# Where the mixers' PSUM banks lie, and how their first normed tiles are placed

## The chip, the cores and the metric

The kernel runs on one core of one Trainium2 chip. The metric is the device time of one execution in microseconds (us), here the median of three runs. Engines are named as in the profile: PE (TensorE matmuls, PEld their weight loads), DVE (VectorE), ACT (ScalarE), POOL (GpSimd), SP (SyncE, which here issues almost all DMAs).

## The reference

One decoder block over 1040 tokens (16 meta tokens and 1024 of the input) of width 1024: a half-step SwiGLU feed-forward, a mixer stage, a second half-step SwiGLU, a final norm.

```python
h = h + 0.5 * _swiglu(_rmsnorm(h, ffn1_norm[l]), ffn1_w_gu[l], ffn1_w_down[l])
u = _rmsnorm(h, mix_norm[l])
aq, ak, av, az, abeta, aalpha, bcols, ga, gb = jnp.split(u @ w_in[l], _offsets(IN_SIZES), axis=-1)
o_a = _deltanet_branch(...)
o_b = _rwkv7_branch(...)
merged = jax.nn.sigmoid(ga) * o_a + jax.nn.sigmoid(gb) * o_b
h = h + merged @ w_out[l]
h = h + 0.5 * _swiglu(_rmsnorm(h, ffn2_norm[l]), ffn2_w_gu[l], ffn2_w_down[l])
return _rmsnorm(h, final_norm)[:, N_META:]
```

The two branches are a gated DeltaNet in chunks and an RWKV-7 time mixing, with 8 and 16 heads.

## The kernel before

Activations lie transposed: 8 tiles h0 to h7 of 128 features by 1040 tokens. Every matrix product is made of three fp32r products: each operand is split into a high part (ACT copies it, line 163) and a low part (a subtraction, line 164, on DVE unless another engine is named), and high x high, high x low and low x high are summed in PSUM. The order of instructions on each engine is fixed at compile time by a list scheduler with its own timing model; an engine then executes its queue strictly in order, waiting on semaphores.

**First feed-forward, ffn1.** The down products go through 7 rounds r of Strassen-like forms. A round has 11 forms (a `form` tile: 128 x 520, high and low part), loaded from the DRAM buffer frm, and 4 products m (pd, line 707), each added to h by DVE (line 714). `Hidden` keeps a list `slots` of the places in which the 77 forms lie in turn. `even` and `odd` are places in the buffers of the gate-up stage (11, 21, t2 and t3, 22, t4, t1: four each). The last round (r = 6) is made in two passes, first 264 columns of all four m, then 256. `before_last`, called after round 5, loads that round's last forms into the freed weight-sum buffer wsum, loads the constants ck, and opens on the right side of SBUF the pools `up` (the mixers' inputs uk) and `un` (norm temporaries). `after` runs behind each product of the last round: squares and their sums for the mixers' norm, of segment 0 (528 tokens: nsq summed on DVE) and segment 1 (512 tokens: nsq summed on POOL). After the first pass the segment-0 sum is reduced by a matmul with ones (nps, line 338) and becomes the scale nrs (lines 340 and 341, ACT). Behind each product of the second pass, two tiles nt = h * gain * nrs (line 871, DVE) are made and split into uk (lines 163 and 164): the low part on POOL for odd k, on DVE for even k.

**Mixers, middle.** PSUM has 8 banks. ffn1 has `mm` with 3 pairs of banks (0 to 5) for products and `mx` with banks 6 and 7. `middle` closes these, opens `ch` with two banks (for the chains of a head pair, and for the head pair's final norms: cs, lines 1213 to 1234), and then `main_banks` opens `mm` and `mx` in what is left: 2 pairs and 2 banks, later, from the seventh head pair on, 3 single banks and 3. Memory is allocated from the lowest address unless a pool says `side="right"`; with `reuse_waits="tile"` a new tile waits for the users of whatever lay in its place. The first projections (pp, line 307) take the eight uk in order, for 272 columns and then 256. POOL clears the mixers' buffers (line 1006 on), behind its ffn1 work.

**Between the mixers and the second feed-forward, ffn2.** `fill` makes the output product (pwo, line 307; ho, line 1101) of the first half while the last head pair is still in its chains, and splits seven of the second half's eight inputs (uk from mr). The eighth comes from `finish` of the last head pair: cs of oa and yb, ro and rg (ACT), yb, uk. Then `ffn2` opens `mm` with 6 banks and `mx` with 2 and makes the second half's pwo, each weight tile of which lies in one of two buffers (tag "w"), in the course of its own first norm (nsq, lines 320 and 327).

Of the kernel before, what the change touches and what calls it, by code (L numbers as in the profile page):

```python
# [8 lines left out]
F32 = mybir.dt.float32  # L9
F32R = mybir.dt.float32r  # L10
# [3 lines left out]
P = 128  # L14
D = 1024
KD = D // P
# [8 lines left out]
ROW = lambda n: -(-n // 64) * 64  # L25
# [16 lines left out]
HK = KD // 2  # L42
HF = NF // 2
# [4 lines left out]
LAST = len(FORMS) - 1  # L48
# [62 lines left out]
def build(tc, nc, a):  # L111

    ctx = ExitStack()
    with ctx:
# [39 lines left out]
        ffn1(g)  # L154
        middle(g)
        ffn2(g)


# [216 lines left out]
def first_half(g, hs, gname, n, b, on_pe):  # L375

    src = lambda k: hs[k][:, :n]
    rs = rstd(g, src, n, on_pe)
    yield
    for k in range(KD):  # L380
        g.nc.vector.scalar_tensor_tensor(src(k), src(k), g.V(gname, k), rs, op0=ALU.mult, op1=ALU.mult)
        bk = b["21" if k >= HK else "11"][:, k % HK]
        split(g, src(k), bk[:, 0, :], bk[:, 1, :])
    yield
# [89 lines left out]
def weight_tiles(g):  # L474

    new = lambda pool, name, k: pool.tile([P, 2, k, P], F32R, name=name, tag=name)
    g.wq = [g.wp.tile([P, 2, KD, P], F32R, name="w", tag="w", bufs=WB) for _ in range(2)]
    g.wq += [new(g.wx, "w22", HK), new(g.wx, "w22b", HK), new(g.wx, "w24", KD)]
# [143 lines left out]
class Hidden:  # L622
# [46 lines left out]

    def arrange(self, spare, last):  # L670
        e, o = self.even, self.odd
        self.slots = e[:HF] + (o[:HF] + e[:HF]) * 2 + o[:HF] + o[HF:] + [spare] + last

    def load(self, upto, done):
        while len(self.loads) < min(upto, len(self.slots)):
# [93 lines left out]
def ffn1(g):  # L769
    tc, nc = g.tc, g.nc  # L770
    n = T // 2
    with ExitStack() as ctx:
        right = ExitStack()
        early = ExitStack()
        pools = {}
        for names, pool in ((("11", "21", "t2"), early.enter_context(
                tc.tile_pool(name="f1a", bufs=1, side="right", reuse_waits="tile"))),
                (("t3", "22", "t4", "t1"), ctx.enter_context(tc.tile_pool(name="f1b", bufs=1, reuse_waits="tile")))):
            pools.update({x: pool for x in names})
        b = {x: p.tile([P, HK, 2, ROW(n)], F32R, name=f"b{x}", tag=f"b{x}", bufs=1)[:, :, :, :n]  # L780
             for x, p in pools.items()}
        b["12"] = b["t4"]
        g.wx = right.enter_context(tc.tile_pool(name="wx", bufs=1, side="right", reuse_waits="tile"))
        g.ga = right.enter_context(tc.tile_pool(name="ga", bufs=1, side="right", reuse_waits="tile"))
        with tc.tile_pool(name="f1n", bufs=1, reuse_waits="tile") as sp:
            hs = [sp.tile([P, T], F32, name=f"h{k}") for k in range(KD)]
            for s in range(2):
                for k in range(KD):
                    sl = slice(s * n, (s + 1) * n)
                    (nc.sync if s or k % 2 else nc.scalar).dma_start(hs[k][:, sl], g.a["hT"][k][:, sl])  # L790
                if not s:
                    weight_tiles(g)
                    q0 = whole(g, 1, 0, 0, g.wq[0], g.wq[1])
                    w0 = next(q0)
            q1 = whole(g, 1, 0, 1, g.wq[4], g.wq[2], g.wq[3])
            w1 = next(q1)
            first = first_half(g, hs, "g1", n, b, True)
            next(first)
            next(q0)
            next(first)  # L800
            next(q0)
            start(g, 1, hs, "g1", n, b, (w0, w1), q1)
            gu = g.gate_up
        hidden = Hidden(g, n, pools, 1)
        wp = ctx.enter_context(tc.tile_pool(name="ws", bufs=1, reuse_waits="tile"))
        g.wsum = wp.tile([P, HK, HF, P], F32, name="wsum", tag="wsum", bufs=1)
        with tc.tile_pool(name="gs", bufs=1, reuse_waits="tile") as sp:
            gu.send((hidden.ahead(), sp))
        right.close()
        xctx = ExitStack()  # L810
        sp = ctx.enter_context(tc.tile_pool(name="f1", bufs=1, reuse_waits="tile"))
        hs = {k: sp.tile([P, T], F32, name=f"h{k}") for k in (3, 7, 2, 6, 5, 1, 0, 4)}
        spare = sp.tile([P, 2, ROW(n)], F32R, name="form")[:, :, :n]
        hidden.odd = hidden.places("t3", "22", "t4", "t1")
        hidden.arrange(spare, [])
        g.wthird = ctx.enter_context(tc.tile_pool(name="wd", bufs=1, reuse_waits="tile"))
        hooks = K()

        def residual(k, half):
            sl = slice(half * n, half * n + n)  # L820
            in_turn(g, hs[k][:, sl], g.a["hT"][k][:, sl])

        hooks.before = lambda r, m: residuals(r, m, residual)

        def before_last():
            early.close()
            t = wp.tile([P, 5, 2, ROW(n)], F32R, name="form", tag="wsum", bufs=1)
            hidden.slots += [t[:, i, :, :n] for i in range(5)]
            hidden.load(len(hidden.slots), LAST)
            for x in ("t3", "22"):  # L830
                t = pools[x].tile([P, 3, 2, CHUNKS[0][1], P], F32R, name="w", tag=f"b{x}", bufs=1)
                g.held += [t[:, i] for i in range(3)]
            g.upctx = ExitStack()
            cp = g.upctx.enter_context(tc.tile_pool(name="ckp", bufs=1, side="right", reuse_waits="tile"))
            g.ck = cp.tile([P, NSB - P + 32], F32, name="ck")[:, : NSB - P]
            in_turn(g, g.ck, g.a["ck"][:, P:NSB])
            g.up = g.upctx.enter_context(tc.tile_pool(name="up", bufs=1, side="right", reuse_waits="tile"))
            g.un = xctx.enter_context(tc.tile_pool(name="un", bufs=1, side="right", reuse_waits="tile"))
            with ExitStack() as after:
                for x in g.silus:  # L840
                    after.enter_context(tc.issue_after(x.ins))
                nc.scalar.preload_act_table_set("natural_log_exp_and_others")
            hooks.rms = [Rms(g, lambda: g.un.tile([P, 528], F32, name="nsq", tag="nsq", bufs=4), n,
                             add_on=nc.gpsimd if s else None) for s, (_, n, _) in enumerate(SEGS)]
            hooks.todo = []
            for s in range(2):
                for k in range(HK, KD):
                    squares(s, k)

        def squares(s, k):  # L850
            t0, sn, _ = SEGS[s]
            hooks.rms[s].add(hs[k][:, t0 : t0 + sn])
            nc.sync.dma_start(g.hdr[s][k], hs[k][:, t0 : t0 + sn])

        def after(r, m, s):
            if r < LAST:
                if r == LAST - 1 and m == HK - 1:
                    before_last()
                return
            squares(s, m)  # L860
            if m == HK - 1:
                rs = g.un.tile([P, 528], F32, name="nrs", tag="nrs", bufs=2)
                hooks.rms[s].finish(rs)
                if s == 0:
                    g.u = []
                    hooks.todo = [(k, rs) for k in range(KD)]
                else:
                    nc.sync.dma_start(g.rdr, rs[:, :FULL])
            for k, rs in hooks.todo[: 2 * s]:
                t = g.un.tile([P, 528], F32, name="nt", tag="nt", bufs=2)  # L870
                nc.vector.scalar_tensor_tensor(t, hs[k][:, SEGS[0][0] :], g.V("gm", k), rs, op0=ALU.mult, op1=ALU.mult)
                g.u.append(u_tile(g, t, nc.gpsimd if k % 2 else None))
            del hooks.todo[: 2 * s]

        hooks.after = after
        down(g, hs, 1, n, hidden, hooks)
        xctx.close()


def ffn2(g):  # L880
    tc, nc = g.tc, g.nc
    n = FULL
    main_banks(g, 1, 6, 8)
    with ExitStack() as ctx:
        right = ExitStack()
        bp = ctx.enter_context(tc.tile_pool(name="f2b", bufs=1, reuse_waits="tile"))
        pools = {x: bp for x in ("11", "21")}
# [25 lines left out]
        hidden = Hidden(g, n, pools, 2)  # L913
# [7 lines left out]
        g.wthird = ctx.enter_context(tc.tile_pool(name="wd", bufs=1, reuse_waits="tile"))  # L921
        hidden.odd = hidden.places("t3", "22", "t4", "t1")
        e = hidden.even
        hidden.arrange(e[HF], e[4:9])
        hooks = K()
        hooks.rows = {}

# [55 lines left out]
def middle(g):  # L983
    tc, nc = g.tc, g.nc
    g.mmctx.close()
    with ExitStack() as ctx:
        g.ch = ctx.enter_context(tc.tile_pool(name="ch", bufs=2, space=bass.MemoryType.PSUM, reuse_waits="tile"))
        ctx.callback(g.mmctx.close)
        ep = lambda name, bufs=1: ctx.enter_context(tc.tile_pool(name=name, bufs=bufs, reuse_waits="tile"))
        g.ms = ep("ms")  # L990
# [86 lines left out]
def u_tile(g, src, eng=None):  # L1077

    n = src.shape[-1]
    uk = g.up.tile([P, 2, ROW(528)], F32R, name="uk", tag="uk", bufs=8)[:, :, 528 - n : 528]  # L1080
    split(g, src, uk[:, 0, :], uk[:, 1, :], eng)
    return uk
# [836 lines left out]
```

## Time and profile before

| | us |
|---|---|
| median of three runs | 3006.02 (3003.01 to 3011.42) |
| profiled execution | 3009.62 |
| its span on the core | 3007.6 |
| ffn1 | 0 to about 708 |
| mixers | about 714 to 2290 |
| ffn2 | about 2290 to 3008 |

The view of stretches (busy time of each engine, then the mean granted clock of PE, the share of the DMA engines and GB/s) puts the passages beside the long stages:

```profile
690.00:735.00 45.00, 38.28 (x283) 36.44 (x282) 28.45 (x33) 22.36 (x35) 20.58 (x29) 0.89 0.31 98
...
870.00:1485.00 615.00, 589.54 (x7374) 508.03 (x7373) 472.59 (x1193) 353.01 (x738) 31.60 (x136) 0.99 0.30 77
...
2220.00:2350.00 130.00, 122.25 (x872) 95.20 (x871) 73.86 (x124) 52.90 (x85) 0.93 (x2) 0.95 0.56 176
```

In a line of the timeline stand start, duration, engine, line, operation, output and inputs, shapes and count; in brackets the idle time before it and the instruction that ended the wait. Instructions of one line that follow each other are merged. Releasers are inferred.

### The profile page before, as it was taken

The page shows a single profiled execution, that of the slowest core. Times are in us where ns is not written, and L with a number is a line of the kernel's source. Part 1 is how long each engine was busy: PE and PEld are TensorE (multiplying, and loading weights), DVE is VectorE, ACT ScalarE, POOL GpSimd, SP SyncE. Part 2 cuts the span into 40 slices and gives each one's busy share as a digit, 9 for nine tenths or more (in the row PEclk, how much of TensorE's full clock was granted, in tenths as well). Part 3 has the DMA queues.
Part 4 walks back from the last instruction along what each step waited for, and adds up shares of the span by engine and source line. Part 5 has one row for each costly group of instructions (what it writes and reads, how often), then busy time and mean ns, then how long its engine had stood idle before and what let it go on. Part 6 is the DMA issues. An engine that isn't in the chain of part 4 may idle for free.

```text
span 3007.6 us, 62829 instructions
## 1 busy us (share of the span) xinstructions
PE 2890.0 (96%) x25630; PEld 2501.7 (83%) x25630; DVE 2194.8 (73%) x4079; ACT 1445.0 (48%) x2546; POOL 491.2 (16%) x554
## 2 busy tenths in 40 slices
PE   8999999998989999999998999999998999999998
PEld 8999999998878888888776777777776888888886
DVE  7566668776667877788767887777866666667886
ACT  5322234345655656566566656656644432223444
POOL 0332332323000000000000100100100033332531
PEclk9999999999999999999999999999999999999999
DMA  3433236453232322333332332233354333333762
GB/s 123 134 107 106 93 122 210 170 193 111 74 74 66 83 72 64 81 82 87 93 90 71 81 82 75 74 84 86 106 148 158 114 109 103 100 104 132 248 226 95
DMA packets 286849, 333.14 MB, mean 111 GB/s; under 512 B 172432, under 2 KB 178576, under 8 KB 286560
## 3 DMA queue, kind: packets, MB, share of 16 engines
q1 hardware_dynamic: 284752, 325.77, 35.7%
q8 instruction: 201, 3.29, 0.5%
q10 hardware_dynamic: 1728, 3.16, 0.3%
q14 instruction: 88, 0.72, 0.1%
q0 software_dynamic: 80, 0.19, 0.0%
HBM read 261.67 MB, written 67.38 MB: 109 GB/s over the span
## 4 chain that ended last, share of the span: by engine, by line
PE 50%; DVE 12%; ACT 5%; issue 2%; DMA 1%; SPq 0%; POOL 0%; DVEq 0%; ACTq 0%
PE pp L307 16%; PE pg L494 11%; PE pd L707 6%; PE pwo L307 3%; DVE w L164 2%; DVE tb L1581 1%; PE pg L518 1%; DVE Xb L1583 1%; ACT w L163 1%; PE cs L1213 1%; PE vp L1266 1%; PE mp L1266 1%; DVE mt L1689 1%; PE gra L1467 1%; PE np L1266 1%
## 5 line engine op out<-in xcount | busy, mean ns | idle before, releaser
L307 PE MATMUL pp<-uk,w 128*128 128x512 f32 (+2 forms) x4824 | 969.8, 347 | 15.2 <-DVE h L714 6.0
L307 PEld LDWEIGHTS pp<-uk,w 128*128 128x128 f32 x4824 | 744.0, 191 | 111.9 <-DVE w L164 13.1
L707 PE MATMUL pd<-form,w 128*128 128x256 f32 (+2 forms) x2772 | 437.2, 320 | 9.9 <-DVE w L164 9.2
L707 PEld LDWEIGHTS pd<-form,w 128*128 128x128 f32 x2772 | 396.7, 190 | 49.9 <-DVE w L164 12.3
L494 PE MATMUL pg<-bt,w 128*128 128x256 f32 (+2 forms) x2520 | 401.7, 318 | 2.5 <-DVE w L164 2.0
L164 DVE TENSOR_TENSOR w<-wraw,w 128x1024 fp32r<-128x1024 f32 (+2 forms) x266 | 349.2, 1313 | 74.9 <-ACT w L163 71.8
L494 PEld LDWEIGHTS pg<-bt,w 128*128 128x128 f32 x2520 | 360.2, 188 | 36.4 <-DVE w L164 3.1
L163 ACT ACTIVATE w<-wraw 128x1024 fp32r<-128x1024 f32 (+2 forms) x266 | 276.5, 1040 | 191.5 <-PE pg L494 116.1
L500 DVE TENSOR_TENSOR c<-c,pg 128x520 f32<-128x520 f32 (+1 forms) x280 | 189.5, 689 | 240.0 <-PE pg L494 216.0
L494 PE MATMUL pg<-b,w 128*128 128x256 f32 (+2 forms) x2160 | 347.9, 318 | 0.0
L494 PEld LDWEIGHTS pg<-b,w 128*128 128x128 f32 x2160 | 309.8, 188 | 28.0
L163 ACT ACTIVATE w<-wrx 128x1024 fp32r<-128x1024 f32 (+1 forms) x64 | 58.4, 912 | 280.4 <-PE pg L494 238.5
L464 POOL TENSOR_TENSOR wrx<-wrx 128x512 f32<-128x512 f32 x38 | 52.5, 1382 | 727.0 <-DVE w22b L164 549.8
L164 DVE TENSOR_TENSOR form<-form 128x520 fp32r<-128x520 f32 (+1 forms) x152 | 145.1, 991 | 13.0 <-ACT form L163 12.7
L163 ACT ACTIVATE w<-wsum 128x768 fp32r<-128x768 f32 x96 | 75.7, 788 | 160.3 <-PE pd L707 120.9
L164 DVE TENSOR_TENSOR w<-wsum,w 128x768 fp32r<-128x768 f32 x96 | 116.0, 1214 | 36.8 <-ACT w L163 36.8
L1583 DVE TENSOR_TENSOR Xb<-Xb,tb 115x126 f32<-115x126 f32 (+22 forms) x496 | 125.8, 254 | 8.9 <-DVE tb L1581 0.2
L163 ACT ACTIVATE form<-form 128x520 fp32r<-128x520 f32 (+1 forms) x152 | 94.2, 632 | 77.1 <-DMA form<-frm 67.7
L1581 DVE TENSOR_TENSOR tb<-Ub,Xb 115x126 f32<-115x126 f32 (+22 forms) x496 | 124.5, 251 | 8.4 <-DMA Ub<-scr 1.2
L242 POOL TENSOR_TENSOR wsum<-wsum,wraw 128x768 f32<-128x768 f32 (+1 forms) x48 | 96.3, 2020 | 209.7 <-DMA wraw<-in_wdn 122.1
L1390 DVE SCALAR_TENSOR_TENSOR acc<-xr,pk,acc 128x528 f32<-128x528 f32 (+1 forms) x144 | 108.9, 757 | 28.5 <-ACT acc L1386 28.0
L307 PE MATMUL pwo<-uk,w 128*128 128x512 f32 x384 | 99.5, 412 | 4.1 <-DVE w L164 1.9
(424 smaller groups left out, 4391.3 us busy)
## 6 DMA issues: line engine op xcount, KB each, us to landing
wraw<-in_win SPq DMA_DIRECT2D x150, 512.0 KB
wraw<-in_wgu SPq DMA_DIRECT2D x44, 512.0 KB
wrx<-in_wgu SPq DMA_DIRECT2D x44, 512.0 KB
frm<-c SPq DMA_DIRECT2D x76, 260.0 KB
form<-frm SPq DMA_DIRECT2D x76, 260.0 KB
frm<-c SPq DMA_DIRECT2D x76, 256.0 KB
form<-frm SPq DMA_DIRECT2D x76, 256.0 KB
wraw<-in_wdn SPq DMA_DIRECT2D x40, 384.0 KB
```

The lines of the kernel that those rows point to most:

```text
L163: g.nc.scalar.activation(hi, src, AF.Copy)
L164: (eng or g.nc.vector).tensor_tensor(lo, src, hi.bitcast(F32), op=ALU.subtract)
L242: g.nc.gpsimd.tensor_tensor(s, x, y, op=ALU.add if r == 1 else ALU.subtract)
L307: g.nc.tensor.matmul(ps, lhsT=l, rhs=r, start=i == 0, stop=i == n - 1)
L464: sums.tensor_tensor(a22, a21, a22, op=ALU.add)
L494: nc.tensor.matmul(ps[:, c0 : c0 + cn], lhsT=l[:, x, k, :], rhs=r[:, k, y, c0 : c0 + cn], start=i == 0, stop=i == 3 * HK - 1)
L500: nc.vector.tensor_tensor(o, x, y, op=ALU.add)
L707: nc.tensor.matmul(pd[:, c0 : c0 + cn], lhsT=wd[:, u, k - k0, :], rhs=x[:, v, c0 : c0 + cn], start=k + i == 0, stop=k == HF - 1 and i == 2)
L1266: g.nc.tensor.matmul(ps[e][HS[dst], c0 : c0 + CB], lhsT=l, rhs=r, start=True, stop=True)
L1390: nc.vector.scalar_tensor_tensor(acc[:, :n], xr[:, tap : tap + n], V("convw", ct * 4 + tap), acc[:, :n], op0=ALU.mult, op1=ALU.add)
L1581: nc.vector.tensor_tensor(tv, U[:, i, i + 1 :].unsqueeze(2).to_broadcast([npt, nt, ncc]), X[:, i, 0:ncc].unsqueeze(1).to_broadcast([npt, n ...
L1583: nc.vector.tensor_tensor(X[:, i + 1 :, 0:ncc], X[:, i + 1 :, 0:ncc], tv, op=ALU.add)
```

## The change

Four edits. (1) `ch` moves to the top of PSUM, so that `mm` and `mx` of the mixers begin at bank 0. (2) The eight nt tiles get eight places, in the buffer t4 of ffn1, instead of two in `un`. (3) The form that had its place in t4 (the first of the last round) is no longer there; the last round's forms move up one place, and the eleventh gets a new tile in `un`, loaded after ck. In ffn2 a further place of `even` takes that part. (4) The low part of the eighth uk is made by DVE instead of POOL, which makes three (k = 1, 3, 5).

```diff
     def arrange(self, spare, last):
         e, o = self.even, self.odd
-        self.slots = e[:HF] + (o[:HF] + e[:HF]) * 2 + o[:HF] + o[HF:] + [spare] + last
+        self.slots = e[:HF] + (o[:HF] + e[:HF]) * 2 + o[:HF] + o[-HK:] + [spare] + last
...
             hidden.slots += [t[:, i, :, :n] for i in range(5)]
             hidden.load(len(hidden.slots), LAST)
+            hooks.nt = pools["t4"].tile([P, KD, 528], F32, name="nt", tag="bt4", bufs=1)
...
             g.un = xctx.enter_context(tc.tile_pool(name="un", bufs=1, side="right", reuse_waits="tile"))
+            hidden.slots += [g.un.tile([P, 2, ROW(n)], F32R, name="form")[:, :, :n]]
+            hidden.load(len(hidden.slots), LAST)
...
             for k, rs in hooks.todo[: 2 * s]:
-                t = g.un.tile([P, 528], F32, name="nt", tag="nt", bufs=2)
+                t = hooks.nt[:, k]
                 nc.vector.scalar_tensor_tensor(t, hs[k][:, SEGS[0][0] :], g.V("gm", k), rs, op0=ALU.mult, op1=ALU.mult)
-                g.u.append(u_tile(g, t, nc.gpsimd if k % 2 else None))
+                g.u.append(u_tile(g, t, nc.gpsimd if k in (1, 3, 5) else None))
...
-        hidden.arrange(e[HF], e[4:9])
+        hidden.arrange(e[HF], e[4:10])
...
-        g.ch = ctx.enter_context(tc.tile_pool(name="ch", bufs=2, space=bass.MemoryType.PSUM, reuse_waits="tile"))
+        g.ch = ctx.enter_context(tc.tile_pool(name="ch", bufs=2, space=bass.MemoryType.PSUM, side="right", reuse_waits="tile"))
```

## The prediction

> **What bounds the kernel now.** I read the page's first two parts first. TensorE (PE) is busy nearly all of the span, at a granted clock of 1 nearly everywhere, so time can only come from the few places where it stands still.
>
> ```profile
> PE 2890.0 (96%) x25630; PEld 2501.7 (83%) x25630; DVE 2194.8 (73%) x4079; ACT 1445.0 (48%) x2546; POOL 491.2 (16%) x554
> ```
>
> The change touches the passage from the first feed-forward block into the mixers, so next comes the timeline of PE there, and of the engines that feed it (start, duration, engine, line, idle time before and its releaser).
>
> ```profile
> 694.12 14.15 PE L707 MATMUL pd<-form,w 128*128 128x256 f32 x115
> 714.23 2.83 PE L307 MATMUL pp<-uk,w 128*128 128x272 f32 x11 [5.96 <-DVE h L714]
> 717.83 2.08 PE L338 MATMUL nps<-nsq,ones 128*128 128x512 f32 x2 [0.76 <-POOL nsq L327]
> 718.92 16.31 PE L307 MATMUL pp<-uk,w 128*128 128x272 f32 x122
> ...
> 708.67 0.41 DVE L714 SCALAR_TENSOR_TENSOR h<-pd,h 128x256 f32<-128x256 f32 x1
> 709.73 3.40 DVE L871 SCALAR_TENSOR_TENSOR nt<-h,pk,nrs 128x528 f32<-128x528 f32 x2
> 713.06 0.70 DVE L164 TENSOR_TENSOR uk<-nt,uk 128x528 fp32r<-128x528 f32 x1
> 713.67 0.41 DVE L714 SCALAR_TENSOR_TENSOR h<-pd,h 128x256 f32<-128x256 f32 x1
> ...
> 709.50 1.35 POOL L164 TENSOR_TENSOR uk<-nt,uk 128x528 fp32r<-128x528 f32 x1 [2.00 <-ACT uk L163]
> 713.89 1.30 POOL L164 TENSOR_TENSOR uk<-nt,uk 128x528 fp32r<-128x528 f32 x1 [1.32 <-ACT uk L163]
> 715.14 1.37 POOL L1006 MEMSET Y<- 128x1536 f32 x1
> 716.47 1.30 POOL L327 TENSOR_TENSOR nsq<-nsq 128x512 f32<-128x512 f32 x1
> ...
> 714.18 0.63 ACT L320 ACTIVATE nsq<-h 128x512 f32<-128x512 f32 x1
> 724.89 0.70 ACT L1126 ACTIVATE wa<-pp,pk 128x528 f32<-128x528 f32 x1 [3.60 <-PE pp L307]
> ```
>
> The last product of the feed-forward block ends at 694.12 + 14.15 = 708.27. The first projection, pp, needs nothing of it, but starts only after VectorE (DVE) has added that product to h at 713.67 to 714.08: its PSUM bank is the product's. DVE had the add behind normed tiles nt and low parts uk. Then 11 pp matmuls run, and PE, which works in order, stops for the nps sum, whose input GpSimd (POOL) adds at 716.47, behind the eighth low part (713.89) and a memset. Stretches of that time (PE, PEld, DVE, ACT, POOL busy, then the granted clock) show the second price:
>
> ```profile
> 710.00:711.00 1.00, 0.00 (x0) 0.00 (x0) 1.00 (x1) 0.00 (x0) 1.00 (x2) 0.78 0.63 244
> 720.00:721.00 1.00, 1.00 (x7) 1.00 (x7) 0.00 (x0) 0.97 (x2) 1.00 (x2) 0.60 0.00 0
> ```
>
> The clock halves about two us into the idle time and is back only near 720.6. ACT reads the first projection at 724.89, 16.6 us after 708.27; its 48 matmuls at 16.31/122 = 0.134 and the two nps at full clock, half of 2.08, are 7.5. So some 9 us are lost here.
>
> The PSUM edit also reaches the other end of the mixers, where the second feed-forward block takes all eight banks. PE, DVE and ACT there, then one stretch:
>
> ```profile
> 2284.86 0.63 PE L1213 MATMUL cs<-hl,onesr 128*128 128x512 f32 x2
> 2288.58 1.68 PE L1213 MATMUL cs<-hl,bdr 128*128 128x512 f32 x2 [3.09 <-ACT hl L1227]
> 2291.04 18.38 PE L307 MATMUL pwo<-uk,w 128*128 128x512 f32 x73 [0.78 <-ACT rg L1232]
> ...
> 2279.62 0.69 DVE L1101 TENSOR_TENSOR ho<-pwo,ho 128x512 f32<-128x512 f32 x1 [1.47 <-PE pwo L307]
> 2281.86 3.69 DVE L164 TENSOR_TENSOR uk<-mr,uk 128x512 fp32r<-128x512 f32 x6
> 2286.15 1.22 DVE L164 TENSOR_TENSOR w<-wraw,w 128x1024 fp32r<-128x1024 f32 x1
> 2287.52 0.69 DVE L164 TENSOR_TENSOR uk<-mr,uk 128x512 fp32r<-128x512 f32 x1
> 2295.37 0.69 DVE L164 TENSOR_TENSOR uk<-yb,uk 128x512 fp32r<-128x512 f32 x1 [0.70 <-ACT uk L163]
> 2299.44 1.23 DVE L164 TENSOR_TENSOR w<-wraw,w 128x1024 fp32r<-128x1024 f32 x1 [3.38 <-ACT w L163]
> 2300.58 3.06 DVE L327 TENSOR_TENSOR nsq<-nsq 128x512 f32<-128x512 f32 x4
> ...
> 2298.35 1.06 ACT L163 ACTIVATE w<-wraw 128x1024 fp32r<-128x1024 f32 x1 [3.01 <-PE pwo L307]
> 2299.31 2.70 ACT L320 ACTIVATE nsq<-hh 128x512 f32<-128x512 f32 x5
> ...
> 2292.00:2294.00 2.00, 2.00 (x6) 1.56 (x5) 1.90 (x4) 0.00 (x0) 0.00 (x0) 0.50 1.09 362
> ```
>
> The output products pwo of the second half wait for ACT's rg, from which they take no data; rg reads bank 0, which the ch pool has, and the built program gives the first pwo bank 0 too. Six of its eight inputs are there by 2285.55, the seventh at 2288.21, its weights earlier. PE waits 3.09 us, then 0.78, and still runs at half clock from 2292 to 2294.
>
> **The change, part by part.** *Banks, at the opening.* With ch at the top, the projections start at bank 0. In the built program before, the block's last four products lie in the pairs of banks from 2, 0, 4 and 2, and the first projection in the pair from 2, which is the wait that the trace shows. Bank 0 is the second product's, added to h before 708.67. The wait for the last add goes. What is late next are the eight uk: pp takes them in order, three matmuls each per half.
>
> *Eight places and the low parts.* nt had two places; now DVE can make all eight ahead. What the places can give shows in the mean durations from 696.5 to 715.2 (by form), beside the shortest ones (min/median/max in ns):
>
> ```profile
> L871 DVE SCALAR_TENSOR_TENSOR nt<-h,pk,nrs 128x528 f32<-128x528 f32 x8 | 8.7, 1124 | 0.1
> L164 DVE TENSOR_TENSOR uk<-nt,uk 128x528 fp32r<-128x528 f32 x4 | 4.9, 1229 | 0.0
> ...
> L871 DVE SCALAR_TENSOR_TENSOR nt<-h,pk,nrs x8: 752/762/1795, 697.5 to 711.3; 128x528 f32<-128x528 f32 x8
> L164 DVE TENSOR_TENSOR uk<-nt,uk x4: 694/1196/1830, 701.1 to 713.1; 128x528 fp32r<-128x528 f32 x4
> L164 POOL TENSOR_TENSOR uk<-nt,uk x4: 1304/1572/2307, 700.0 to 713.9; 128x528 fp32r<-128x528 f32 x4
> ```
>
> DVE has practically no idle time here (0.1 before nt, 0.0 before uk), so the two places cost it nothing as it stands; it loses time while POOL works: nt 1.12 for 0.75, uk 1.23 for 0.69, some 3 + 2 us. So I count the places at 0, and the eighth low part at 0.69 more on DVE against 1.30 less on POOL: it is ready about 713.76 + 0.69 = 714.4 instead of 715.19, and POOL is free for nsq at once. If the last add of h follows it (714.9), ACT's square (0.63) and POOL's add (1.30) put nps at about 717.0 instead of 717.83. Meanwhile PE has done the matmuls of uk 0 to 5 or more, 18 to 24 instead of 11, but has then been idle from about 711.5: the clock falls again. From 717.0 the way to the projection's end is the old 724.89 - 717.83 = 7.06, less 7 to 13 matmuls of which most ran at half clock (0.26, as 2.83/11): 1.6 to 2.6. The projection ends 2.4 to 3.4 earlier. I take **-2.8**. Bounds: 0, if order on DVE or POOL eats it; -5.2, if PE never waits for nps and keeps its clock (uk 7 at 714.4, then 27 matmuls at 0.134 and 1.0 for nps, 719.1, and some 0.6 until ACT, an estimate).
>
> [...]
>
> *The memsets.* They follow on POOL in either case and overlap PE; PE waits for none of them, so 0.
>
> *Banks, at the end of the mixers.* The lowest banks now were the mixers' own pwo banks, emptied by the add at 2279.62 (ending 2280.31); the upper ones have been idle. If the first pwo gets the lowest bank again, PE can start at 2285.5 and fill the wait for hl. Seven inputs of two products are 42 matmuls of 18.38/73 = 0.25, at most 10.5 us, and with cs they reach 2296, when uk 7 is there (2296.06 now, some 0.3 sooner with cs at full clock). Cover ends there: both weight tiles are in use until then. The third is split from about 2296.9, ready 2.3 later as now (2298.35 to 2300.67), at 2299.2. Now the third product starts near 2291.04 + 48 x 0.25 = 2303, 2303.7 with the slow start. That is -4.5; half an us may be lost behind DVE and ACT, whose norm work is just as long. I take **-4.0**, between 0 and -5.4 (3.09 + 0.78 and half of 3.2 us at half clock).
>
> *The eleventh form of the last round.* Its place moves from t4, loaded early, to a tile that is loaded after ck. SP's queue, one stretch (its last number is GB/s) and the first user of what follows:
>
> ```profile
> 662.51 2.46 SPq L223 DMA_DIRECT2D form<-frm  x5
> 665.07 0.38 SPq L223 DMA_DIRECT2D ck<-in_ck  x1
> 666.84 4.93 SPq L223 DMA_DIRECT2D wraw<-in_wdn  x2
> ...
> 671.00:672.00 1.00, 1.00 (x11) 1.00 (x10) 1.00 (x2) 0.00 (x0) 0.00 (x0) 1.00 1.07 417
> ...
> 673.68 0.85 ACT L163 ACTIVATE w<-wraw 128x768 fp32r<-128x768 f32 x1 [3.12 <-DMA wraw<-in_wdn]
> ```
>
> One more load of the size of the five (128 x 520 x 4 bytes, 266 KB) at 417 GB/s delays the weight load behind it by 0.64 us, and ACT waits for that load. PE has no idle time there now, so part is hidden: **+0.5**, from 0 to 1.5 (that, and ACT's hi part in front of the weight's). In the second block the same edit replaces one free place by one long released; 0.
>
> Sum: -2.8 - 4.0 + 0.5 = -6.3. From the profiled 3009.6 that is 3003.3; the median of the three runs, 3006.0, lies 3.6 lower, so 2999.7, say **3000**.
>
> **The rivals.** [...]
>
> *A new wait replaces the old one at the opening:* nps stands as early in PE's order as now and the last add stays last on DVE: opening -0.5, the rest -3; with the form 3003.
>
> *Slower:* at the second block two products hold both weight tiles until uk 7. If the scheduler puts the five squares (2.70) and four adds (3.06) ahead of the third weight's split, it is ready at 2299.2 + 5.8 = 2305, PE idles 7 us and restarts at half clock (about 3 lost): +4.3 against now. It decides from 2303.7 on, the third product's present start. With the opening at -0.5 and the form at +1.5: +5.3, 3011.
>
> *The change does not do what it says:* the order of a statically scheduled program shifts elsewhere and hides both gains; about 3006.
>
> **How the numbers follow.** Forecast 0.47, both vanish 0.20, new wait 0.18, slower 0.09, nothing 0.06. A measurement of this kernel tells 0.3%, 9 us, from no change. Below 2997 lies half of the second case and a quarter of the first: faster 0.24; slower than 3015 only the tail of the slower one, 0.04; within 0.72. The range takes in all but the extremes, 2993 to 3010.
>
> **What would show it.** Right: pp starts within an us of 708.3; nt and uk on DVE keep means near 1.1 and 1.2; nps starts near 717; pwo starts by 2286, and the rg wait is gone. Wrong: a wait for DVE h before pp, PE idle beyond 2300 for a w split, a stall near 673 to 678 for form, or a middle that runs more than 2 us longer or shorter between the two passages.

## The result, and the profile after

| | before | changed |
|---|---|---|
| median, us | 3012.36 (3003.01 to 3018.53, 20 executions) | 3002.91 (2993.68 to 3011.16, 20 executions) |
| ratio, 95% interval | | 0.9974 (0.9965 to 0.9983) |
| span of the profiled execution | 3007.6 | 2999.5 |

The change makes the kernel 0.26% faster, some 8 us, with an interval from 5 to 11. The median of the three runs known ahead, 3006.02, is the second lowest of the 20 of before, and 6.3 us under their median.

First the opening of the mixers, from the last product pd of ffn1 to the copy wa that ends the first projection, in the changed kernel: PE's timeline, then that of DVE, ACT and POOL (start, duration, engine, line, idle time before and what ended it). Lines 874, 1009 and 1129 are the former 871, 1006 and 1126.

```profile
702.82 1.00 PE L707 MATMUL pd<-form,w 128*128 128x256 f32 x7
703.66 1.52 PE L307 MATMUL pp<-uk,w 128*128 128x272 f32 x11
711.72 2.08 PE L338 MATMUL nps<-nsq,ones 128*128 128x512 f32 x2 [6.54 <-POOL nsq L327]
712.80 9.38 PE L307 MATMUL pp<-uk,w 128*128 128x272 f32 x54
...
706.02 1.76 DVE L874 SCALAR_TENSOR_TENSOR nt<-h,pk,nrs 128x528 f32<-128x528 f32 x1
708.49 0.71 DVE L164 TENSOR_TENSOR uk<-nt,uk 128x528 fp32r<-128x528 f32 x1 [0.71 <-ACT uk L163]
709.12 0.42 DVE L714 SCALAR_TENSOR_TENSOR h<-pd,h 128x256 f32<-128x256 f32 x1
...
709.63 0.63 ACT L320 ACTIVATE nsq<-h 128x512 f32<-128x512 f32 x1 [0.95 <-DVE h L714]
720.12 0.70 ACT L1129 ACTIVATE wa<-pp,pk 128x528 f32<-128x528 f32 x1 [4.94 <-PE pp L307]
...
710.40 1.26 POOL L327 TENSOR_TENSOR nsq<-nsq 128x512 f32<-128x512 f32 x1 [1.87 <-ACT nsq L320]
```

The wait for DVE's add ahead of pp, 5.96 us before, is gone: pp follows pd without a gap. But PE does 11 pp matmuls, as before, and then stands 6.54 us at nps. The chain that nps waits for is plain: DVE's last add (709.12 to 709.54), ACT's square (to 710.26), POOL's add (to 711.66), nps. The add has the place that it had, last on DVE, behind eight nt and five low parts. From the last pd (703.80) to the copy wa that ends the first projection there are 16.32 us; before there were 16.64.

The clock explains why so little came of it. These are stretches of 3.41 us of the changed kernel's PE (length, busy us and matmuls, granted clock, DMA share, GB/s):

```profile
704.04:707.45 3.41, 1.14 (x10) 1.00 0.20 77
707.45:710.86 3.41, 0.00 (x0) 0.50 0.14 52
710.86:714.27 3.41, 2.55 (x5) 0.50 0.07 27
714.27:717.68 3.41, 3.41 (x17) 0.50 0.35 118
```

PE's idle time is hardly shorter (6.54 us for 5.96 + 0.76); it lies later against the end of pd, from 1.4 to 7.9 us behind it instead of from 0 to 6.0. The clock comes back 6 us after PE resumes, so of the 8.40 us from nps to wa, in which 37 projection matmuls and nps run, 5.98 are at half clock; before, nps to wa took 7.06, of which 2.97 were at half clock.

Now the passage to ffn2 of the changed kernel, PE and then ACT:

```profile
2282.39 0.62 PE L1216 MATMUL cs<-hl,onesr 128*128 128x512 f32 x2
2282.85 2.45 PE L307 MATMUL pwo<-uk,w 128*128 128x512 f32 x10
2285.99 0.50 PE L1216 MATMUL cs<-hl,bdr 128*128 128x512 f32 x1 [0.69 <-ACT hl L1230]
2286.33 0.86 PE L307 MATMUL pwo<-uk,w 128*128 128x512 f32 x3
2287.02 0.39 PE L1216 MATMUL cs<-hl,bdr 128*128 128x512 f32 x1
2287.25 16.27 PE L307 MATMUL pwo<-uk,w 128*128 128x512 f32 x67
...
2314.09 0.73 PE L307 MATMUL pwo<-uk,w 128*128 128x512 f32 x2 [3.12 <-ACT w L163]
2315.04 1.15 PE L307 MATMUL pwo<-uk,w 128*128 128x512 f32 x2 [0.22 <-ACT w L163]
2316.74 8.60 PE L307 MATMUL pwo<-uk,w 128*128 128x512 f32 x26 [0.55 <-DVE w L164]
...
2294.04 1.06 ACT L163 ACTIVATE w<-wraw 128x1024 fp32r<-128x1024 f32 x1 [1.54 <-PE pwo L307]
2295.88 1.06 ACT L163 ACTIVATE w<-wraw 128x1024 fp32r<-128x1024 f32 x1 [0.78 <-PE pwo L307]
2296.84 3.41 ACT L320 ACTIVATE nsq<-hh 128x512 f32<-128x512 f32 x6
...
2312.99 1.99 ACT L163 ACTIVATE w<-wraw 128x1024 fp32r<-128x1024 f32 x2
```

pwo now starts right behind cs; the waits of 3.09 us for hl and 0.78 us for rg have become one of 0.69. The third product's first matmul comes 13.29 us behind cs, for 18.73 before. Of these 5.4 us 1.7 are given back, 0.55 of it at 2314, where two weight splits are late (ACT makes them at 2312.99): 3.12 + 0.22 + 0.55 us of waits, for 1.48 + 1.86 before, where the same matmuls read:

```profile
2320.06 0.73 PE L307 MATMUL pwo<-uk,w 128*128 128x512 f32 x2 [1.48 <-ACT w L163]
2322.65 23.88 PE L307 MATMUL pwo<-uk,w 128*128 128x512 f32 x92 [1.86 <-DVE w L164]
```

From cs to the last pwo matmul it is 57.53 us, for 61.28 before: 3.75 saved.

The sum of what is seen, 0.3 + 3.75, is half of the 8.1 us between the two spans. A difference as large as the rest lies ahead of the opening. From the first pd of ffn1 to the start of its last round both kernels issue the same 1584 matmuls in the same order, and the changed kernel's trace is 4.5 us shorter there. Its third edit does move one load of a form there (it is issued at 660.98 now), but the 4.5 can't be put down to that: three traces of the changed kernel itself (e4_again and e13_control, below, are the other two) take 193.7, 196.1 and 202.3 us for that stretch, for 198.2 before. Over the fourteen traces of this study it takes 190.9 to 202.8 us: 197.0 on average with the third edit (ten traces), 198.6 without it (four), which the spread doesn't tell apart. So a difference of a few us between two spans says nothing of a change; differences below are read from the stretch concerned, and whole times from ratios.

### The profile page after: what moved, and what is told of

Same layout as the page of the kernel before. It is cut to its first block, busy times and chain, and to the rows that moved or that the text cites. A ratio compares the mean times of both kernels' runs of the same rounds, so it can differ in the third digit from the quotient of the medians.

```text
span 2999.5 us, 62835 instructions
## 1 busy us (share of the span) xinstructions
PE 2886.0 (96%) x25630; PEld 2497.4 (83%) x25630; DVE 2189.7 (73%) x4080; ACT 1445.4 (48%) x2546; POOL 491.9 (16%) x553
## 3 DMA queue, kind: packets, MB, share of 16 engines
q1 hardware_dynamic: 284752, 325.77, 35.6%
## 5 line engine op out<-in xcount | busy, mean ns | idle before, releaser
L494 PEld LDWEIGHTS pg<-bt,w 128*128 128x128 f32 x2520 | 360.1, 188 | 37.1 <-DVE w L164 3.1
```

The source lines that it names most:

```text
L494: nc.tensor.matmul(ps[:, c0 : c0 + cn], lhsT=l[:, x, k, :], rhs=r[:, k, y, c0 : c0 + cn], start=i == 0, stop=i == 3 * HK - 1)
```

## The experiments

Each run was set beside the kernel before on its own chip; the ratios are to that. The stretches in this table are read from the traces, in us: from the end of the last pd matmul of ffn1 to the end of DVE's last add of h, to the start of nps of segment 1 (where it is made of two matmul pairs, of the second), and to the start of wa; how long PE was granted half clock there (by stretches of 0.1 us); and from the start of the last head pair's first cs matmul to that of the last pwo matmul.

| kernel | last add | nps | wa | half clock | cs to last pwo | median | ratio (95%) |
|---|---|---|---|---|---|---|---|
| before | 5.83 | 9.57 | 16.64 | 10.2 | 61.28 | | |
| changed | 5.74 | 7.92 | 16.32 | 10.2 | 57.53 | 3002.91 | 0.9974 (0.9965 to 0.9983) |
| e1_banks | 5.81 | 9.54 | 17.00 | 6.8 | 56.99 | 3007.45 | 0.9992 (0.9982 to 1.0002) |
| e2_places | 5.72 | 8.50 | 14.23 | 6.8 | 60.84 | 3005.16 | 0.9988 (0.9974 to 1.0002) |
| e4_again | 5.77 | 7.95 | 16.14 | 6.8 | 57.22 | 3004.87 | 0.9978 (0.9966 to 0.9991) |
| e6_ffn2_banks | 5.81 | 9.55 | 17.73 | 10.3 | 56.91 | 3005.97 | 0.9984 (0.9971 to 0.9997) |
| e3_four_low | 4.32 | 8.66 | 15.80 | 6.8 | 57.06 | 3004.30 | 0.9975 (0.9961 to 0.9989) |
| e5_add_first | 1.62 | 4.46 | 11.80 | 3.4 | 57.02 | 3002.60 | 0.9967 (0.9953 to 0.9982) |
| e8_last_on_pe | 1.61 | 2.39 | 9.03 | 0 | 56.63 | 2998.93 | 0.9956 (0.9941 to 0.9970) |
| e9_places_ffn2 | 5.71 | 8.49 | 14.69 | 6.8 | 56.57 | 3005.06 | 0.9980 (0.9965 to 0.9995) |
| e10_chain_ch_low | 1.62 | 2.40 | 9.03 | 0 | 56.50 | 2993.65 | 0.9947 (0.9931 to 0.9963) |
| e11_chain_two_places | 2.49 | 3.27 | 11.04 | 0 | 56.98 | 3001.52 | 0.9976 (0.9964 to 0.9988) |
| e12_pe_sum_alone | 5.70 | 6.47 | 15.74 | 6.9 | 57.75 | 3001.60 | 0.9979 (0.9970 to 0.9988) |
| e13_control | 5.72 | 7.91 | 16.01 | 6.9 | 57.07 | 3003.70 | 0.9982 (0.9971 to 0.9993) |

The medians of before beside them were 3010.13 (e1, e2, e4, e6), 3012.32 (e3, e5, e8, e9) and 3009.05 (e10 to e13). Most runs have 12 executions, e8_last_on_pe 9 and e10_chain_ch_low 6.

**The change taken apart: e1, e2, e4, e6.** e1_banks is the kernel before with the first edit alone.

```diff
-        g.ch = ctx.enter_context(tc.tile_pool(name="ch", bufs=2, space=bass.MemoryType.PSUM, reuse_waits="tile"))
+        g.ch = ctx.enter_context(tc.tile_pool(name="ch", bufs=2, space=bass.MemoryType.PSUM, side="right", reuse_waits="tile"))
```

> Only edit 1 (ch at the top of PSUM); nt keeps two places, four low parts on POOL. Theory A (nearly all of the gain lies at the passage to ffn2, where the first pwo no longer shares a bank with cs; the opening gives nearly nothing, since nps still waits for POOL's last nsq): from the end of cs to the third output product 4 us less, first pp within an us of the last pd, nps still some 9 us behind the last pd, first projection 16 us behind it, total -3 to -6 us (ratio 0.998 to 0.999). Rival B (places and low parts carry a good half): total -2 or less.

The passage to ffn2 has its whole gain; the opening has none. PE's timeline there:

```profile
709.44 1.53 PE L307 MATMUL pp<-uk,w 128*128 128x272 f32 x11
719.12 2.08 PE L338 MATMUL nps<-nsq,ones 128*128 128x512 f32 x2 [8.15 <-POOL nsq L327]
```

The wait for the bank is gone and its time, 5.96 + 0.76 before, stands at nps as 8.15, since the 11 matmuls took 1.53 at full clock instead of 2.83 at half. In whole time the kernel fell short of what was expected: 0.9992, with an interval that takes in 1, for 0.998 to 0.999.

e2_places is the other way round: edits 2 to 4, with `ch` lowest.

```diff
-        g.ch = ctx.enter_context(tc.tile_pool(name="ch", bufs=2, space=bass.MemoryType.PSUM, side="right", reuse_waits="tile"))
+        g.ch = ctx.enter_context(tc.tile_pool(name="ch", bufs=2, space=bass.MemoryType.PSUM, reuse_waits="tile"))
```

(This diff is against the changed kernel.)

> Edits 2, 3 and 4 without edit 1 (ch stays lowest). Theory A: first pp waits for the last add of h again, pwo waits for rg again; DVE stays saturated, nt near 1.1 us; total 0 to -2 us (ratio 0.9995 to 1.0005). Rival B: -3 to -6 us.

Its PE:

```profile
711.50 2.83 PE L307 MATMUL pp<-uk,w 128*128 128x272 f32 x11 [5.85 <-DVE h L714]
714.13 1.21 PE L338 MATMUL nps<-nsq,ones 128*128 128x512 f32 x2
```

With eight places and three low parts on POOL, POOL is ready with the last add while PE does its 11 matmuls at half clock, so nps has no wait. PE resumes 5.87 us behind the last pd, the clock is back 3.0 us later, and wa comes at 14.23. In the changed kernel PE resumes for good at 7.92. That the passage here keeps its old 60.84 shows that its gain belongs to the first edit. The whole time, 0.9988, lies where theory B had it and not theory A (0.9995 to 1.0005); but its interval takes in 1 and all of that of e1_banks, so whole times don't divide the gain between the edits, and only the stretches do.

e4_again is the changed kernel itself, unchanged.

> The changed kernel once more, for a second trace and the ratio on this chip. Theory A: passage to ffn2 4 us shorter, from last pd to first projection 16.3 as in the first trace, rounds 0 to 5 of ffn1 (same program in both) anywhere between the two traces already seen, which differ by 4.5 us there; ratio 0.997 to 0.999. If rounds 0 to 5 are short in this trace too, more than chance makes them short.

It repeats the changed kernel in the stretches (wa 16.14, passage 57.22); the half clock is shorter, 6.8 us for 10.2, but begins later, 6.6 us behind the last pd for 3.7, and so 5.5 us of it lie behind PE's restart at nps, for 6.0.

e6_ffn2_banks is the kernel before with only ffn2's pools placed from the other end.

```diff
-def main_banks(g, w, n, banks=6):
+def main_banks(g, w, n, banks=6, side="left"):
...
-        g.tc.tile_pool(name=name, bufs=bufs, space=bass.MemoryType.PSUM, reuse_waits="tile"))
+        g.tc.tile_pool(name=name, bufs=bufs, space=bass.MemoryType.PSUM, side=side, reuse_waits="tile"))
...
-    main_banks(g, 1, 6, 8)
+    main_banks(g, 1, 6, 8, "right")
```

> The kernel before, with only ffn2's pools turned round (mm takes banks 2 to 7, mx 0 and 1), so that its first pwo lies in a bank that the mixers' mm had. Theory A: the opening as before (16.6 us from the last pd to the first projection), pwo starts right behind the first cs, 4 us less at that passage, total -3 to -5 us (ratio 0.9985). Rival: the time found there is lost again in ffn2's norm, ratio 0.9995 to 1.0.

Passage 56.91: a bank of ffn2's own choice does there all that moving `ch` does. The opening is as before up to nps (9.55); from there wa comes 1.1 us later than in the trace of before (17.73): PE is at half clock from 4.8 to 15.0 us behind the last pd, in the trace of before from 2.3 to 12.5.

**The chain to nps: e5 and e8.** If the opening ends with DVE's last add, square, sum and nps, then what shortens this chain must show at once. e5_add_first is the changed kernel with every nt and uk put behind the add to h of the product just made.

```diff
-            nc.vector.scalar_tensor_tensor(hv, pd[:, c0 : c0 + cn], 0.5, hv, op0=ALU.mult, op1=ALU.add)
+            g.added = nc.vector.scalar_tensor_tensor(hv, pd[:, c0 : c0 + cn], 0.5, hv, op0=ALU.mult, op1=ALU.add)
...
-                t = hooks.nt[:, k]
-                nc.vector.scalar_tensor_tensor(t, hs[k][:, SEGS[0][0] :], g.V("gm", k), rs, op0=ALU.mult, op1=ALU.mult)
-                g.u.append(u_tile(g, t, nc.gpsimd if k in (1, 3, 5) else None))
+                with tc.issue_after(g.added.ins):
+                    t = hooks.nt[:, k]
+                    nc.vector.scalar_tensor_tensor(t, hs[k][:, SEGS[0][0] :], g.V("gm", k), rs, op0=ALU.mult, op1=ALU.mult)
+                    g.u.append(u_tile(g, t, nc.gpsimd if k in (1, 3, 5) else None))
```

> The changed kernel, with VectorE's normed tiles of the first segment put behind the adds to h of the second segment's products, so that the last add is no longer last on VectorE. Theory A (the opening is set by the chain VectorE's last add, ScalarE's square, GpSimd's add, nps, and the matmuls ahead of nps only move the idle time): the last add ends 0.5 to 2.5 us behind the last pd matmul instead of 5.7, nps starts 4 to 6 us behind it instead of 7.9, the first projection's copy comes 12 to 14 us behind it instead of 16.3; the whole 2 to 4 us below the changed kernel on the same chip. Theory B (VectorE and GpSimd share the tiles' work, whose sum sets uk 7, and the order is indifferent): uk 7 later by 1 to 2 us and the first projection's copy still 15.5 to 17 us behind the last pd matmul, time within 1 us of the changed kernel.

The rows of the last add, nps and wa (line 1130 here):

```profile
713.27 0.41 DVE L714 SCALAR_TENSOR_TENSOR h<-pd,h 128x256 f32<-128x256 f32 x1
...
716.53 1.27 PE L338 MATMUL nps<-nsq,ones 128*128 128x512 f32 x2 [3.21 <-POOL nsq L327]
...
723.86 0.70 ACT L1130 ACTIVATE wa<-pp,pk 128x528 f32<-128x528 f32 x1 [4.46 <-PE pp L307]
```

They come 1.62, 4.46 and 11.80 behind the last pd, wa a little sooner than expected. The last tile was ready 1.0 us later than in the changed kernel (6.39 for 5.40 behind the last pd), and that cost nothing: behind nps PE doesn't wait for it. Theory A holds in the stretches: the order on DVE, not the sum of its work, set the opening. In whole time, 0.9967 is not told from the changed kernel's 0.9974 to 0.9982.

e8_last_on_pe adds to e5 that PE itself sums the last square, with a second matmul into nps.

```diff
-            squares(s, m)
+            last = None
+            if s and m == HK - 1:
+                t0, sn, _ = SEGS[s]
+                last = hs[m][:, t0 : t0 + sn]
+                nc.sync.dma_start(g.hdr[s][m], last)
+            else:
+                squares(s, m)
             if m == HK - 1:
                 rs = g.un.tile([P, 528], F32, name="nrs", tag="nrs", bufs=2)
-                hooks.rms[s].finish(rs)
+                hooks.rms[s].finish(rs, last)
```

> As the run with the adds ahead, and the last square of the second segment is summed by TensorE (a second matmul into nps) and not by GpSimd. Theory A: GpSimd's add of 1.4 us leaves the chain, nps's second matmul costs 2.1 us more at the reduced clock but starts behind 3 projection matmuls instead of 10: it starts 3 to 4.5 us behind the last pd matmul, PE has under 3 us idle there in all, and the first projection's copy comes 11 to 13 us behind the last pd matmul; the whole 0 to 2 us below the run with the adds ahead. Theory B (uk 7 sets the end): the copy comes no sooner than in the run with the adds ahead, since the first product ends behind uk 7 in both; time equal within 1 us or 1 us above for the extra matmul.

PE in this kernel, then ACT's copy of the first projection (line 1136 here):

```profile
713.16 1.13 PE L338 MATMUL nps<-nsq,ones 128*128 128x512 f32 x2
713.72 0.94 PE L307 MATMUL pp<-uk,w 128*128 128x272 f32 x3
715.40 1.13 PE L338 MATMUL nps<-nsq,ones 128*128 128x512 f32 x2 [0.74 <-ACT nsq L320]
715.96 7.29 PE L307 MATMUL pp<-uk,w 128*128 128x272 f32 x55
...
722.04 0.70 ACT L1136 ACTIVATE wa<-pp,pk 128x528 f32<-128x528 f32 x1 [2.92 <-PE pp L307]
```

The scheduler has also put nps behind 3 projection matmuls here, where it stood behind 10 in e5. PE stands 0.74 us at nps, the clock doesn't fall in the opening, and wa comes 9.03 us behind the last pd, 7.3 sooner than in the changed kernel. That is sooner than expected by either theory; theory A still counted nps at the reduced clock. Against before the whole is 0.9956: about 13 us, of which the opening's 7.6 and the passage's 4.65 are seen in its trace.

**Low parts and the two gains together: e3 and e9.** e3_four_low undoes the fourth edit.

```diff
-                g.u.append(u_tile(g, t, nc.gpsimd if k in (1, 3, 5) else None))
+                g.u.append(u_tile(g, t, nc.gpsimd if k % 2 else None))
```

> The changed kernel with four low parts of the normed tiles on GpSimd again (the last, number 7, too). Theory A: VectorE has one low part less, 0.6 to 1.1 us, so its last add of h ends 0.5 to 1 us sooner, but GpSimd has one of 1.2 to 1.5 us more ahead of the last squares' add, so nps comes 0 to 1 us later; first projection's copy 16 to 17.5 us behind the last pd matmul; time 0 to 1 us above the changed kernel, inside the interval. Theory B (the three low parts are where a gain of the opening lies): nps 1.5 us later or more, and 2 us or more slower than the changed kernel.

DVE's last add comes 1.4 us sooner and nps 0.7 us later, because POOL has the eighth low part ahead of the last sum. The copy wa comes at 15.80, for 16.0 to 16.3 in the changed kernel, and the time is that of the changed kernel; the place of one low part only moves the wait between two links of the chain.

e9_places_ffn2 is e2 with e6's placing in ffn2.

> The kernel before with the eight places, the three low parts on GpSimd and the eleventh form, the mixers' two accumulators still lowest in PSUM, and the second ffn's two pools placed from the other end (so that its first product needs no bank of the accumulators). Theory A (the two gains seen apart, opening -2.4 and the passage to the second ffn -4.0 to -4.4, add): first projection's copy 14 to 14.5 us behind the last pd matmul, the accumulators' last matmul to the end of the first 80 products of pwo 57 us; 5.5 to 7.5 us below before, ratio 0.9975 to 0.9982, and 1 to 3 us below the changed kernel. Theory B (the opening's gain in one trace was run to run and does not add): first projection's copy 16 to 17 us behind the last pd matmul, and time equal to the changed kernel and to the run with the second ffn's pools alone, ratio 0.9982 to 0.999.

wa at 14.69 and the passage at 56.57: the two parts add in one trace. In whole time, 0.9980 (0.9965 to 0.9995) is neither told from the changed kernel nor from e6; the 1 to 3 us below the changed kernel that theory A expected are not seen.

**What is left once the chain is short: e10 to e13.** e10_chain_ch_low is e8 with `ch` lowest and ffn2's pools from the other end, so that the first projection must wait for the last add again.

> The kernel with the adds ahead and the last square summed by TensorE, but with the mixers' accumulators lowest in PSUM again and the second ffn's pools placed from the other end, so that the first projection again waits for VectorE's last add of h and the passage to the second ffn keeps its gain. Theory A (once the chain of the last squares is short, PE's early start on the projections is worth only the wait for the last add): the first projection's first matmul 1.6 to 2.2 us behind the last pd matmul, nps's second half 3 to 4 us behind it, PE without half clock in the opening, the first projection's copy 9.5 to 10.5 us behind the last pd matmul against 9.0; time 0 to 1.5 us above the run with that chain and the changed banks. Theory B (the early start itself carries the gain of that run): copy 12 us behind or later, time 3 us or more above it.

It waits 0.49 us, and wa comes at 9.03, exactly as in e8:

```profile
710.45 1.13 PE L338 MATMUL nps<-nsq,ones 128*128 128x512 f32 x2
712.06 0.61 PE L307 MATMUL pp<-uk,w 128*128 128x272 f32 x3 [0.49 <-DVE h L714]
712.69 1.13 PE L338 MATMUL nps<-nsq,ones 128*128 128x512 f32 x2
713.25 17.73 PE L307 MATMUL pp<-uk,w 128*128 128x272 f32 x141
```

So with a short chain the mixers' place in PSUM brings nothing at the opening. This is the fastest kernel of the study: 0.9947 (0.9931 to 0.9963, six executions), 10 us under the changed kernel on the same chip. That it is under e8 too was expected by neither theory, no stretch of the traces shows it, and the intervals overlap.

e11_chain_two_places is e8 without edits 2 to 4.

> The changed banks, the adds ahead and the last square summed by TensorE, with the two places, four low parts on GpSimd and ten forms of the kernel before (edits 2 to 4 of the change left out). Theory A (with two places the normed tiles are served one after the other, but nothing on PE waits for them until the later steps of the first product): the last add 1.6 to 3 us behind the last pd matmul, the last tile 7 to 9 us behind it, the first projection's copy 9.5 to 12 us behind; time 0.5 to 3 us above the run with the eight places. Theory B (the places are indifferent): copy at 9 us, time equal within 0.5 us.

With two places and four low parts on POOL the last tile is ready 7.55 us behind the last pd instead of 5.38, PE waits 0.56 us for POOL's uk, and wa comes 2.0 later than in e8. So edits 2 to 4 together are worth 2 us here. The medians put e11 8 us above e10, more than this stretch accounts for; that stays open.

e12_pe_sum_alone is the changed kernel with e8's second half only, DVE's order left as it is.

> The changed kernel with the last square of the second segment summed by TensorE, and VectorE's order as in the changed kernel. Theory A (VectorE's last add, 5.7 us behind the last pd matmul, is the head of the chain, and GpSimd's add is only its tail): nps's second half 6.5 to 7.2 us behind the last pd matmul (7.9 in the changed kernel), PE idle 4.5 to 5.5 us, half clock again, the first projection's copy 14 to 16 us behind; time 0.3 to 2 us below the changed kernel. Theory B (GpSimd's add is the head): nps 3 to 5 us behind, copy 9 to 12 us behind, time 4 us or more below the changed kernel.

nps comes at 6.47, the clock halves, wa at 15.74: POOL's sum is only the tail of the chain, DVE's add its head.

e13_control is the changed kernel again, on the chip of e10 to e12.

> The changed kernel once more, on the chip of the three runs beside it. Theory A: nps 7.9 us and the first projection's copy 14 to 17 us behind the last pd matmul, in between by the phase of the clock alone (how many stretches of 3.4 us at half clock); ratio to before 0.997 to 0.9985; 6 to 9 us above the run with the short chain. Theory B (rival: the changed kernel's opening gains 2 to 3 us in most executions and the two traces seen were the unlucky ones): copy at 13 to 14 us.

wa at 16.01 and nps at 7.91. In three traces of the changed kernel wa stands at 16.32, 16.14 and 16.01, so it was no accident of one execution that the opening gained so little.

## Why the prediction was right, and where not

The total was right: forecast 3000 with a range of 2993 to 3010, 0.2% under before; measured 3002.91 and 0.26%. But it came out in part by luck. Of the 6.3 us forecast, the pair of traces shows some 4 where they were expected; the opening fell short of its term by 2.5, and what the ratio shows beyond these 4 has no known source. The case "both vanish", the bounds -5.2 and -5.4 together, did not come about: PE stands 6.54 us at nps and is granted half clock for 10.2.

- **Banks at the end of the mixers, -4.0: right.** -3.75 in the pair of traces. Kernels with the old placing take 61.28 and 60.84 us for the passage, the twelve with a new one 56.5 to 57.75, 57.0 on average: -4.0. It also went as described: pwo starts by 2286, the rg wait is gone, the third product starts 5.4 us sooner (4.5 was counted), and 1.7 of it is given back (0.5 was). The slower rival did not come about: ACT has the splits of 2294.04 and 2295.88 ahead of its squares, and PE runs through from 2287.25.
- **The opening, -2.8: wrong, -0.3 in the pair** (-1.4 to -1.7 beside e6_ffn2_banks, whose opening is that of before). The first half of the reasoning held: pp starts at once, nps comes 1.65 us sooner behind the last pd (0.8 was counted), the eight tiles are ready sooner than expected (5.40 behind the last pd, for 6.1). The step that failed is "Meanwhile PE has done the matmuls of uk 0 to 5 or more, 18 to 24 instead of 11". PE's order is fixed when the kernel is built, and nps stands in it where it stood, behind 11 matmuls; how much data is ready by then doesn't matter (seven of the eight low parts are there by 706.10, and PE stands at nps until 711.72). With that fell "the old 724.89 - 717.83 = 7.06, less 7 to 13 matmuls": all 37 were still to do, and at half clock for longer (8.40). The opening went as the rival "a new wait replaces the old one" had it, with -0.5. Nor did the edit of banks bring the opening anything in other company: with it alone (e1) wa comes at 17.00, and without it at 14.23 and 14.69 (e2, e9), sooner than with all four edits, though how much of that is the place of the half clock isn't settled.
- **The eleventh form, +0.5: nothing seen.** The last round takes 36.24 us for 36.17 in the pair; over the ten traces with the third edit it is 37.1 on average (35.6 to 38.1), over the four without it 36.9 (36.2 to 37.5). A cost under 0.5 us would not show in these.
- **Places at 0: too little.** The runs tell edits 2 to 4 only together, but for the low part (e3). Beside the first edit they bring little (e1, without them, has wa at 17.00, the changed kernel at 16.0 to 16.3); with `ch` lowest they bring wa from 16.64 to 14.23 and 14.69, part of it perhaps the place of the half clock, and with the short chain 2.0 us (e11 beside e8). The last tile is ready 5.40 behind the last pd, in the trace of before 6.94. DVE's means were expected near 1.1 us for nt and 1.2 for uk and were 1.28 and 1.08, as the groups of the changed kernel by form have them (count, busy us, mean ns, idle time before), from 692 to 710.7:

```profile
L874 DVE SCALAR_TENSOR_TENSOR nt<-h,pk,nrs 128x528 f32<-128x528 f32 x8 | 10.0, 1281 | 0.2 <-ACT nrs L341 0.2
L164 DVE TENSOR_TENSOR uk<-nt,uk 128x528 fp32r<-128x528 f32 x5 | 5.4, 1079 | 0.7 <-ACT uk L163 0.7
```

  Of the 1.5 us by which the last tile is sooner, 1.4 is the start: the first nt begins 12.2 us ahead of the last pd's end, for 10.8 before. From the first nt (691.57) to the last tile (709.20) it is 17.6 us, for 17.7 before. That DVE is slower while POOL works shows here too: the two nt ahead of POOL's first addition (693.70) take 0.76 us each, the six behind it 1.45 on average.
- **The middle.** It was named as a sign of error if it ran over 2 us longer, and in the pair it does (1562.27 us from wa to cs, for 1559.97). The two other traces of the changed kernel have 1559.32 and 1559.44, so it was that execution.
- **Slips in the working.** The clock is back at 720.8, not 720.6. The mean of 0.134 us for a matmul at full clock takes in some at half clock; 141 of them at full clock in e10_chain_ch_low take 17.73, 0.126 each, so that some 0.4 us more were lost at the opening than was counted. The chance of "faster" is 0.22 by its own parts, not 0.24. None of them moves the forecast by half a us.
- **What stays open.** Passage and opening make -4 to -5 us. The three ratios of the changed kernel (0.9974, 0.9978, 0.9982) make -5 to -8. The third's interval takes in -4 and the second's reaches -3; the first's ends at -5. Whether some 1 to 3 us more come from elsewhere, in the mixers or in ffn1's rounds, couldn't be told, since stretches of one and the same kernel differ by more than that between executions.

## What to carry to other kernels

A wait that is removed from an in-order engine is a gain only if the next thing in that engine's queue isn't bound to the same chain (here 5.96 us at pp came back as 6.54 at nps): follow the chain to its head (here an add placed last on DVE) and move that, and count the queue as it was built, not by what data is ready. On PE, early work ahead of a long idle time saved little here (wa at 16.32 for 16.64), since the clock came back only 6.0 us after PE had resumed. And where a pool takes over memory, look at which of the old users sits in its first place: with a false wait there the passage to ffn2 took some 4 us longer here, and placing the pool from the other end removed it (56.91 us in e6_ffn2_banks for 61.28).

## What the hardware showed

In the eleven openings in which half clock was seen, it lasted 3.4 us (e5_add_first), 6.8 to 6.9 (e1, e2, e3, e4, e9, e12, e13) or 10.2 to 10.3 (before, changed, e6). The longest wait of PE did not have the longest half clock: 8.15 us in e1_banks went with 6.8, 5.96 and 0.76 in the kernel before with 10.2. The half clock began 2.0 (e2_places) to 6.6 us (e4_again) behind the last pd.

The stretches of e12_pe_sum_alone show its fall and its return in one opening (columns as above):

```profile
705.57:708.98 3.41, 1.58 (x14) 1.00 0.03 13
708.98:712.40 3.42, 1.50 (x5) 1.00 0.17 64
712.40:715.81 3.41, 2.21 (x4) 0.50 0.21 79
715.81:719.22 3.41, 3.41 (x17) 0.50 0.32 107
```

The clock stayed behind 1.58 busy us of 3.41, fell behind 1.50 and came back behind a full stretch. In such stretches of the other openings it fell behind 1.41 us (e2_places), 1.14 (changed) and less, and stayed behind 1.58 (e4_again), 1.65 (e1_banks), 1.87 (e13_control) and 2.10 (e6_ffn2_banks). In the mixers of the kernel before it went otherwise: the clock fell behind 2.30 busy us and didn't come back behind a full stretch, only behind a second one:

```profile
949.47:952.88 3.41, 2.30 (x48) 1.00 0.00 0
952.88:956.30 3.42, 3.42 (x38) 0.50 0.02 5
956.30:959.71 3.41, 3.41 (x42) 0.50 0.50 154
```

Of the 48 matmuls of the first of these stretches 40 are 32 x 32, in place of 128 x 128. So PE's busy time alone doesn't tell when the clock changes, and what does isn't shown by these traces.

One opening thus varies with where the half clock lies: before and e6_ffn2_banks are alike up to nps (9.57 and 9.55 us behind the last pd), have half clock to 12.5 and to 15.0, and reach wa at 16.64 and 17.73. The difference of 1.7 us between the changed kernel's three traces (16.2 on average) and the two with `ch` lowest (14.2 and 14.7) is not much larger. In those three the half clock ends 13.9, 13.4 and 13.2 us behind the last pd, in these two 8.8 and 9.8; with five traces it isn't settled how much of the difference comes from that.
